# Attention's value product with the values stationary on two halves of the array's columns

## The chip, the cores and the metric

One NeuronCore of a Trainium2 chip runs the kernel. The metric is the device time of one execution in microseconds (us), as a median over several executions. The engines are TensorE (in the rows: PE for matmuls, PEld for weight loads), VectorE (DVE), ScalarE (ACT), GpSimd (POOL) and SyncE (SP, which here issues nearly all DMAs). TensorE's clock has two levels, 1.2 and 2.4 GHz; the rows show the granted share of the full level.

## What is computed

Two layers of a transformer-like block over 256 latent and 256 context tokens, width 1024. Every layer adds the output projection of three groups side by side (a bidirectional gated recurrence, attention, a gated position mixer), then a channel mixer: a dense SwiGLU in the first layer, eight experts, two per token, in the second. The part that is changed is attention with 8 query heads on 2 key-value heads, head size 64, and a sink logit per head:

```python
p = jax.nn.softmax(jnp.concatenate([s_win, s_ctx, s_sink], axis=-1), axis=-1)
p_win = p[..., :n_win].astype(v.dtype)
p_ctx = p[..., n_win:n_win + n_ctx].astype(v.dtype)
o = (jnp.einsum('bnhgqk,bnkhd->bnqhgd', p_win, vw)
     + jnp.einsum('bnhgqc,bchd->bnqhgd', p_ctx, v_ctx))
```

Latent tokens see all context tokens and a window of latent ones; context tokens see context alone, and only the first layer needs their output. All inputs and outputs are f32.

## The kernel before

The kernel is written as Python generators. Each emits instructions for a step and then yields; `run` (line 207) and `weave` (line 223) advance several of them in turn. The emitted order is a priority: a planner of the framework then fixes each engine's queue at compile time, taking by its own estimate what is ready, earlier emitted first. On the chip each queue runs in that order, and semaphores hold what is not yet allowed.

A tile of attention is `attn_tile` (line 1037): 128 query tokens (`tt`) and the four query heads of one key-value head (`g`). Latent tiles have 512 keys in four chunks of 128, context tiles 256 keys in two. Layer 0 has eight tiles: `at0` is group 0 (two context tiles, two latent), `at1` group 1, one after the other, four tiles woven together each. Layer 1 has four, all latent, woven together.

In a tile, each head does this in turn: scores into a PSUM bank (lines 1079 to 1084), the row maximum on VectorE (1085, 1086), Exp with its row sum on ScalarE into the first half of `pt` (1089), the transposes of the head's chunks to another bank (1095), a copy to the second half of `pt` (1097 or 1099), and then one matmul per chunk, with the turned probabilities (128x128) stationary and the values (128x64) moving (1104, by the helper at 1827). The result, tokens by 64 columns a head, collects in `po`. At the end of the tile the four sums are turned to reciprocals (1108 to 1111), `po` is multiplied by them (1114), transposed in two matmuls (1124) and copied into `mix` (1125). f32 matmuls are recorded as two passes each; transposes as one.

Memory of 4 KB per partition is handed out by `Mem` from one first-in-first-out list of 34 slots (`N4`); `room(4, n)` makes a generator yield until n are free. A tile asks for 3 and takes one for `qt`, and for one `pt` per head, which it returns when the head is done. Slots of the recurrence, the output projection and the weight stream come from the same list.

What runs beside the tiles: in layer 0, `hgrn` (the recurrence; its products at line 860 use row halves of the array, its products by decay are lines 849 to 852) and the adaptive-modulation chunks (line 395, four column quarters) run beside `at0`. `filler0` emits the first half of the output projection when recurrence and position mixer are done, and the context half of its second part (`out_proj0`, lines 244 to 246 of `mm3`) when the context tiles are done. In layer 1, `hgrn` runs beside the tiles and `filler1` emits the early output projection (`out_early`) when the recurrence is done and 8 slots are free; `prep_tile` and the expert layer (line 1575) follow. The weights of the experts are prefetched by SP into a ring of slots.

Of the kernel before, what the change touches and what calls it, by code (L numbers as in the profile page):

```python
# [196 lines left out]
class Gen:  # L197
# [839 lines left out]
    def attn_tile(self, l, tt, g):  # L1037
# [32 lines left out]
        pair = (g, tt // 2)  # L1070
        if pair not in st["po"]:
            yield from self.avail("u")
            if pair not in st["po"]:
                st["po"][pair] = [self.psum("u"), 2]
        pb = st["po"][pair]
        po = pb[0][:, 256 * (tt % 2):256 * (tt % 2) + 256]
        for h in range(4):
# [9 lines left out]
            yield from mem.room(4, 1)  # L1087
            pt = mem.get(4, [P, 2, 512], "pp")
            self.act(pt[:, 0, :nk], ps[:, :nk], AF.Exp, bias=nm[:, h:h + 1], accum_out=sm[:, h:h + 1])
            self.done(ps)  # L1090
            yield
            yield from self.avail("t")
            pst = self.psum("t")
            for c in range(nch):
                nc.tensor.transpose(pst[:, c * P:c * P + P], pt[:, 0, c * P:c * P + P], self.ident)
            if h not in PVC[l]:
                self.act(pt[:, 1, :nk], pst[:, :nk], AF.Copy)
            else:
                nc.vector.tensor_copy(pt[:, 1, :nk], pst[:, :nk])
            self.done(pst)  # L1100
            yield
            for c in range(nch):
                vt = st["kv"][:, (k0 // P) + c, 128 + 64 * g:192 + 64 * g]
                self.mm(pb[0], po[:, 64 * h:64 * h + 64], pt[:, 1, c * P:c * P + P], vt, c == 0, c == nch - 1)
            mem.put(pt)
            yield
        mem.put(qt)
        nc.vector.tensor_tensor(es, nm, self.sink[:, l, 4 * g:4 * g + 4], op=ALU.add)
        self.act(es, es, AF.Exp)
        nc.vector.tensor_tensor(es, es, sm, op=ALU.add)  # L1110
        nc.vector.reciprocal(es, es)
        yield from self.mem.room(1, 1)
        o = mem.get(1, [P, 4, 64], "ao")
        nc.vector.tensor_tensor(o, po.rearrange("p (h d) -> p h d", h=4),
                                es[:, :, None].to_broadcast([P, 4, 64]), op=ALU.mult)
        pb[1] -= 1
        if not pb[1]:
            self.done(pb[0])
        yield
        yield from self.avail("t")  # L1120
        pt = self.psum("t")
        of = o.rearrange("p h d -> p (h d)")
# [995 lines left out]
```

## Time and profile before

| | us |
|---|---|
| median of 3 runs | 1839.38 |
| lowest, highest | 1835.87, 1839.55 |
| the profiled execution | 1835.17 |
| its span, first to last instruction | 1833.4 |

The profile is one execution. Its rows give for each group of instructions the busy time and the mean duration of one, for a stretch the busy time of each engine, and in order of time the starts. Durations of matmuls overlap, since the next starts before the last has drained; what a matmul holds TensorE for is read from start to start.

### The profile page before, as it was taken

The page shows a single profiled execution, that of the slowest core. Times are in us where ns is not written, and L with a number is a line of the kernel's source. Part 1 is how long each engine was busy: PE and PEld are TensorE (multiplying, and loading weights), DVE is VectorE, ACT ScalarE, POOL GpSimd, SP SyncE. Part 2 cuts the span into 40 slices and gives each one's busy share as a digit, 9 for nine tenths or more (in the row PEclk, how much of TensorE's full clock was granted, in tenths as well). Part 3 has the DMA queues.
Part 4 walks back from the last instruction along what each step waited for, and adds up shares of the span by engine and source line. Part 5 has one row for each costly group of instructions (what it writes and reads, how often), then busy time and mean ns, then how long its engine had stood idle before and what let it go on. Part 6 is the DMA issues. An engine that isn't in the chain of part 4 may idle for free. (4 is left out here: it accounts for less than half of the span.)

```text
span 1833.4 us, 34728 instructions
## 1 busy us (share of the span) xinstructions
PE 1753.2 (96%) x14056; PEld 1084.3 (59%) x14057; DVE 778.5 (42%) x1924; ACT 537.7 (29%) x1203; POOL 33.3 (2%) x56
## 2 busy tenths in 40 slices
PE   6999999999999999999989998999989999999996
PEld 3999778988788898998843333333333333333332
DVE  4656877899755377868720011110212011120112
ACT  4654655723223256765410010100101011010100
POOL 1000000100000001000000000000000000000000
PEclk9999999999999999999989999999999999999998
DMA  9224342366763245230589999999999999999990
GB/s 347 73 83 147 114 150 80 117 241 226 240 221 134 97 143 182 89 127 13 196 316 379 402 406 407 406 407 400 402 400 406 404 402 402 400 407 404 403 392 31
DMA packets 137006, 485.64 MB, mean 265 GB/s; under 512 B 15888, under 2 KB 17040, under 8 KB 136784
## 3 DMA queue, kind: packets, MB, share of 16 engines
q1 hardware_dynamic: 136080, 480.08, 69.1%
q8 instruction: 168, 2.75, 0.6%
q0 software_dynamic: 704, 2.36, 0.4%
q14 instruction: 54, 0.44, 0.1%
HBM read 481.33 MB, written 1.05 MB: 263 GB/s over the span
## 5 line engine op out<-in xcount | busy, mean ns | idle before, releaser
L1575 PE MATMUL u<-wr,xg 128*32 128x512 f32 (+1 forms) x5376 | 523.9, 545 | 19.7 <-issue 14.6
L1575 PEld LDWEIGHTS u<-wr,xg 128*32 128x32 f32 x5376 | 174.0, 111 | 342.2 <-issue 291.5
L1575 PE MATMUL mm<-wr,mT 128*32 128x512 f32 x2352 | 261.1, 593 | 3.8 <-ACT mh L264 1.5
L125 ACT ACTIVATE hi<-raw 128x512 fp32r<-128x512 f32 (+2 forms) x296 | 160.3, 580 | 247.1 <-PE u L246 84.8
L126 DVE TENSOR_TENSOR lo<-raw,hi 128x512 fp32r<-128x512 f32 (+2 forms) x296 | 178.9, 636 | 98.3 <-ACT hi L125 96.7
L1608 DVE TENSOR_TENSOR mh<-mh,u 128x512 f32<-128x512 f32 (+1 forms) x32 | 19.8, 619 | 410.9 <-PE u L1575 257.0
L1575 PEld LDWEIGHTS mm<-wr,mT 128*32 128x32 f32 x2352 | 77.8, 110 | 175.4 <-issue 149.7
L264 ACT ACTIVATE mh<-u 128x512 f32<-128x512 f32 (+1 forms) x64 | 34.6, 540 | 413.9 <-PE u L1575 413.3
L244 PE MATMUL u<-hx,hi 128*128 128x512 f32 (+1 forms) x384 | 142.9, 372 | 0.0
L245 PE MATMUL u<-hx,lo 128*128 128x512 f32 (+1 forms) x384 | 142.7, 372 | 0.0
L246 PE MATMUL u<-hx,hi 128*128 128x512 f32 (+1 forms) x384 | 142.7, 372 | 0.0
L264 ACT ACTIVATE mT<-t 128x512 f32<-128x512 f32 (+1 forms) x32 | 17.4, 544 | 256.3 <-PE t L1620 255.4
L245 PE MATMUL mm<-fx,lo 128*128 128x256 f32 (+1 forms) x264 | 85.7, 325 | 4.4 <-DVE lo L126 4.2
L244 PE MATMUL mm<-hi,hx 128*128 128x256 f32 x288 | 85.3, 297 | 4.2 <-ACT hx L264 3.9
L244 PE MATMUL mm<-fx,hi 128*128 128x256 f32 (+1 forms) x264 | 85.0, 322 | 0.6 <-ACT hi L125 0.6
L1626 DVE COPY mT<-t 128x256 f32<-128x256 f32 (+1 forms) x32 | 12.5, 392 | 170.6 <-PE t L1625 170.6
L246 PE MATMUL mm<-fx,hi 128*128 128x256 f32 (+1 forms) x264 | 84.6, 321 | 0.0
L245 PE MATMUL mm<-hi,hx 128*128 128x256 f32 x288 | 82.0, 286 | 0.6 <-DVE hx L521 0.3
L246 PE MATMUL mm<-lo,hx 128*128 128x256 f32 x288 | 81.7, 285 | 0.2 <-DVE lo L126 0.2
L246 PEld LDWEIGHTS u<-hx,hi 128*128 128x128 f32 x384 | 72.4, 188 | 12.6
L245 PEld LDWEIGHTS u<-hx,lo 128*128 128x128 f32 x384 | 72.4, 188 | 12.4
L244 PEld LDWEIGHTS u<-hx,hi 128*128 128x128 f32 x384 | 72.4, 188 | 12.4
(342 smaller groups left out, 2624.9 us busy)
## 6 DMA issues: line engine op xcount, KB each, us to landing
wr<-in_moe_g SPq DMA_DIRECT2D x224, 512.0 KB, 10.1
wr<-in_moe_u SPq DMA_DIRECT2D x224, 512.0 KB, 10.1
wr<-in_moe_d SPq DMA_DIRECT2D x224, 512.0 KB, 10.1
adat<-in_w_adaT SPq DMA_DIRECT2D x56, 512.0 KB, 5.0
raw<-in_ffn_gu SPq DMA_DIRECT2D x44, 512.0 KB, 3.5
adaw<-in_w_ada SPq DMA_DIRECT2D x40, 512.0 KB, 6.5
raw<-in_w_in SPq DMA_DIRECT2D x40, 512.0 KB, 3.5
raw<-in_ffn_d SPq DMA_DIRECT2D x24, 384.0 KB, 3.6
```

Of the source, the lines that this page charges most:

```text
L125: nc.scalar.activation(h[:, s], r[:, s], AF.Copy)
L126: nc.vector.tensor_tensor(l[:, s], r[:, s], h[:, s].bitcast(F32), op=ALU.subtract)
L244: i = mm(ps, lh, rh, start=start, stop=False, skip_group_check=True)
L245: mm(ps, ll, rh, start=False, stop=False, skip_group_check=True)
L246: self.final = mm(ps, lh, rl, start=False, stop=stop, skip_group_check=True)
L264: i = self.nc.scalar.activation(out, in_, func, **kw)
L1575: self.nc.tensor.matmul(bank[c:c + 32, :n], lhsT, rhs, start=start, stop=stop, tile_position=(0, c), skip_group_check=True)
L1608: nc.vector.tensor_tensor(h[:, 0, :n], h[:, 0, :n], U[:, :n], op=ALU.mult)
L1626: nc.vector.tensor_copy(hT[:, :m, :, 64:], pt[:, :m * 64].rearrange("p (j a s) -> p j a s", j=m, a=2))
```

## The change

The probabilities are normalised before the product: after every second head the two reciprocals are formed, and GpSimd multiplies the two heads' probabilities by them. The probabilities of all four heads stay (`pp`, two slots). Then, by chunk of keys, the four heads' 128x128 blocks are transposed into one bank and copied to one half of `pT`. After every two chunks two matmuls follow, each with a chunk's values (128x64) stationary and 512 moving columns (four heads by 128 tokens): one on the left half of the array's columns, one on the right, so that even chunks collect in partitions 0 to 63 of `po` and odd ones in 64 to 127. At the end the two halves are added: ScalarE copies each to the other's partitions, VectorE adds, straight into `mix`. The closing multiply and transposes are gone. A tile asks for two slots for `pp` before its first head, returns `qt` after its last and takes one for `pT`, and returns all three at the end. Its steps are 12 turns from the first scores for a latent tile and 9 for a context tile, where both had 14.

```diff
@@ -1067,13 +1067,8 @@
-        pair = (g, tt // 2)
-        if pair not in st["po"]:
-            yield from self.avail("u")
-            if pair not in st["po"]:
-                st["po"][pair] = [self.psum("u"), 2]
-        pb = st["po"][pair]
-        po = pb[0][:, 256 * (tt % 2):256 * (tt % 2) + 256]
+        yield from mem.room(4, 2)
+        pp = [mem.get(4, [P, 2, 512], "pp") for _ in range(2)]
         for h in range(4):
...
-            yield from mem.room(4, 1)
-            pt = mem.get(4, [P, 2, 512], "pp")
-            self.act(pt[:, 0, :nk], ps[:, :nk], AF.Exp, bias=nm[:, h:h + 1], accum_out=sm[:, h:h + 1])
+            p = pp[h // 2][:, h % 2, :nk]
+            self.act(p, ps[:, :nk], AF.Exp, bias=nm[:, h:h + 1], accum_out=sm[:, h:h + 1])
             self.done(ps)
-            yield
+            if h % 2:
+                e = slice(h - 1, h + 1)
+                nc.vector.tensor_tensor(es[:, e], nm[:, e], self.sink[:, l, 4 * g + h - 1:4 * g + h + 1], op=ALU.add)
+                self.act(es[:, e], es[:, e], AF.Exp)
+                nc.vector.tensor_tensor(es[:, e], es[:, e], sm[:, e], op=ALU.add)
+                nc.vector.reciprocal(es[:, e], es[:, e])
+                for i in range(2):
+                    x = pp[h // 2][:, i, :nk]
+                    nc.gpsimd.tensor_scalar(x, x, es[:, h - 1 + i:h + i], None, op0=ALU.mult)
+            yield
+        mem.put(qt)
+        pT = mem.get(4, [P, 2, 512], "pT")
+        yield
+        po = None
+        for c in range(nch):
             yield from self.avail("t")
-            pst = self.psum("t")
-            for c in range(nch):
-                nc.tensor.transpose(pst[:, c * P:c * P + P], pt[:, 0, c * P:c * P + P], self.ident)
-            if h not in PVC[l]:
-                self.act(pt[:, 1, :nk], pst[:, :nk], AF.Copy)
+            ps = self.psum("t")
+            for h in range(4):
+                nc.tensor.transpose(ps[:, h * P:h * P + P], pp[h // 2][:, h % 2, c * P:c * P + P], self.ident)
+            if c not in PVC[l]:
+                self.act(pT[:, c % 2], ps, AF.Copy)
             else:
-                nc.vector.tensor_copy(pt[:, 1, :nk], pst[:, :nk])
-            self.done(pst)
-            yield
-            for c in range(nch):
-                vt = st["kv"][:, (k0 // P) + c, 128 + 64 * g:192 + 64 * g]
-                self.mm(pb[0], po[:, 64 * h:64 * h + 64], pt[:, 1, c * P:c * P + P], vt, c == 0, c == nch - 1)
-            mem.put(pt)
-            yield
-        mem.put(qt)
...
-        nc.vector.tensor_tensor(o, po.rearrange("p (h d) -> p h d", h=4),
-                                es[:, :, None].to_broadcast([P, 4, 64]), op=ALU.mult)
...
-        for j in range(2):
-            nc.tensor.transpose(pt[:, j * P:j * P + P], of[:, j * P:j * P + P], self.ident)
-        self.to_mix(2 * g, tt, pt)
+                nc.vector.tensor_copy(pT[:, c % 2], ps)
+            self.done(ps)
+            yield
+            if c % 2 == 0:
+                continue
+            if po is None:
+                po = yield from self.either("mm", "u")
+            for i in range(2):
+                v = st["kv"][:, (k0 // P) + c - 1 + i, 128 + 64 * g:192 + 64 * g]
+                nc.tensor.matmul(po[64 * i:64 * i + 64], v, pT[:, i], start=c == 1, stop=c == nch - 1,
+                                 tile_position=(0, 64 * i), skip_group_check=True)
+            yield
+        mem.put(pT, *pp)
...
+        for i in range(2):
+            self.act(o[64 * i:64 * i + 64], pv[64 - 64 * i:128 - 64 * i, :, i], AF.Copy)
+        for i in range(2):
+            r = slice(64 * i, 64 * i + 64)
+            nc.vector.tensor_tensor(self.mix[g][r, :, ts], pv[r, :, i], o[r], op=ALU.add)
+        self.done(po)
```

## Rows read from the trace of the kernel before

**Rows 1.** The page, busy time: engine, us, share of the span, instructions.

```profile
PE 1753.2 (96%) x14056; PEld 1084.3 (59%) x14057; DVE 778.5 (42%) x1924; ACT 537.7 (29%) x1203; POOL 33.3 (2%) x56
```

**Rows 2.** Windows with changed tiles: stretch, length, busy by engine; PEclk, DMA share, GB/s.

```profile
213.00:263.00 50.00, 49.37 (x376) 42.20 (x377) 39.80 (x154) 26.22 (x70) 0.56 (x2) 1.00 0.34 115
296.50:322.50 26.00, 25.31 (x204) 23.44 (x203) 19.50 (x64) 21.64 (x65) 0.00 (x0) 1.00 0.18 61
835.60:880.00 44.40, 44.40 (x357) 38.61 (x356) 36.72 (x119) 18.82 (x46) 0.56 (x2) 1.00 0.04 13
880.00:902.50 22.50, 21.80 (x137) 18.66 (x135) 18.29 (x50) 13.69 (x36) 0.00 (x0) 1.00 0.62 219
```

**Rows 3.** Windows: the end of the prefetch, and a stretch of the expert layer.

```profile
930.00:940.00 10.00, 9.23 (x67) 6.27 (x69) 1.11 (x4) 3.49 (x9) 0.00 (x0) 0.95 0.57 227
...
1000.00:1100.00 100.00, 95.61 (x946) 36.52 (x942) 12.07 (x19) 11.30 (x24) 0.00 (x0) 1.00 1.02 402
```

**Rows 4.** Timeline of PE, layer 1: start, us, instructions. Projection, then attention.

```profile
883.80 0.48 PE L244 MATMUL u<-hi,mx 128*128 128x512 f32 x1
...
897.32 1.00 PE L1827 MATMUL u<-akv,pp 128*128 128x64 f32 x8
```

**Rows 5.** The tile `pp`: the value products, ns min/median/max, first and last start.

```profile
L1827 PE MATMUL u<-akv,pp x320: 217/275/323, 220.3 to 901.3; 128*128 128x64 f32 x160
```

**Rows 6.** Timeline of PE: sixteen passes of value products and what follows.

```profile
258.83 2.00 PE L1827 MATMUL u<-akv,pp 128*128 128x64 f32 x16
260.67 0.66 PE L1827 MATMUL u<-S,QC 128*128 128x128 f32 x4
```

**Rows 7.** Timeline of PE: transposes, and products on row halves (L860), apart and together.

```profile
255.34 0.71 PE L860 MATMUL u<-Bl,Al 64*128 64x128 f32 x4
255.98 0.66 PE L1095 MATMUL t<-ident,pp 128*128 128x128 f32 x4
256.56 0.71 PE L860 MATMUL u<-Bl,Al 64*128 64x128 f32 x4
...
859.62 0.72 PE L860 MATMUL u<-Bl,Al 64*128 64x128 f32 x8
860.27 0.50 PE L1079 MATMUL mm<-KT,qt 128*128 128x512 f32 x1
```

**Rows 8.** Timeline of PE in three narrow windows: modulation on four column quarters.

```profile
262.55 0.64 PE L395 MATMUL u<-adaw,sil 128*32 128x512 f32 x4
...
263.00 1.46 PE L395 MATMUL u<-adaw,sil 128*32 128x512 f32 x8
...
263.43 1.03 PE L395 MATMUL u<-adaw,sil 128*32 128x512 f32 x4
```

**Rows 9.** The tile `ao`: the closing multiply, ns min/median/max.

```profile
L1114 DVE TENSOR_TENSOR ao<-u,aes x12: 414/424/426, 259.9 to 901.7; 128x256 f32<-128x256 f32 x12
```

**Rows 10.** Groups by line on POOL: shape, count, busy us, mean ns, idle before.

```profile
L517 POOL TENSOR_TENSOR nt<-X,ny 128x512 f32<-128x512 f32 x4 | 5.0, 1263 | 8.6 <-ACT adas L264 8.6
...
L337 POOL CAST Mf<-cld 128x1024 fp32r<-128x1024 f32 x1 | 1.0, 1042 | 0.9 <-DMA cld<-in_Mf 0.9
```

**Rows 11.** Groups by line on DVE, 835 to 880 us: attention's, and a product by decay.

```profile
L1085 DVE TENSOR_REDUCE anm<-mm 128x1 f32<-128x512 f32 x13 | 8.8, 686 | 0.8 <-PE mm L1083 0.7
L1099 DVE COPY pp<-t 128x512 f32<-128x512 f32 x7 | 4.8, 687 | 1.1 <-PE t L1095 1.0
...
L851 DVE TENSOR_TENSOR Bl<-E,Tq 128x128 f32<-128x128 f32 x11 | 3.2, 289 | 0.0
```

**Rows 12.** Timelines of DVE and POOL, 337.5 to 343.2 us: additions beside POOL.

```profile
338.63 0.96 DVE L477 TENSOR_TENSOR nsq<-nsq 128x256 f32<-128x256 f32 x1
...
342.65 0.41 DVE L477 TENSOR_TENSOR nsq<-nsq 128x256 f32<-128x256 f32 x1
...
338.20 3.58 POOL L517 TENSOR_TENSOR nt<-X,ny 128x256 f32<-128x256 f32 x4 [9.93 <-DVE ny L497]
```

More of the change, by code (lines that the diff above doesn't have):

```diff
@@ new lines, in attn_tile @@
+            yield
[4 more added lines that the diff above has]
+        for c in range(nch):
+            yield from self.avail("t")
+            ps = self.psum("t")
[3 more added lines that the diff above has]
+                self.act(pT[:, c % 2], ps, AF.Copy)
+            else:
+                nc.vector.tensor_copy(pT[:, c % 2], ps)
@@ L1090, in attn_tile @@
             self.done(ps)
             yield
-            yield from self.avail("t")
-            pst = self.psum("t")
-            for c in range(nch):
-                nc.tensor.transpose(pst[:, c * P:c * P + P], pt[:, 0, c * P:c * P + P], self.ident)
-            if h not in PVC[l]:
-                self.act(pt[:, 1, :nk], pst[:, :nk], AF.Copy)
-            else:
-                nc.vector.tensor_copy(pt[:, 1, :nk], pst[:, :nk])
-            self.done(pst)
-            yield
-            for c in range(nch):
-                vt = st["kv"][:, (k0 // P) + c, 128 + 64 * g:192 + 64 * g]
-                self.mm(pb[0], po[:, 64 * h:64 * h + 64], pt[:, 1, c * P:c * P + P], vt, c == 0, c == nch - 1)
@@ L1105, in attn_tile @@
-            mem.put(pt)
-            yield
-        mem.put(qt)
[L1108 to L1113, printed above, removed]
-        nc.vector.tensor_tensor(o, po.rearrange("p (h d) -> p h d", h=4),
-                                es[:, :, None].to_broadcast([P, 4, 64]), op=ALU.mult)
@@ L1116, in attn_tile @@
-        pb[1] -= 1
-        if not pb[1]:
-            self.done(pb[0])
-        yield
-        yield from self.avail("t")
-        pt = self.psum("t")
-        of = o.rearrange("p h d -> p (h d)")
-        for j in range(2):
-            nc.tensor.transpose(pt[:, j * P:j * P + P], of[:, j * P:j * P + P], self.ident)
-        self.to_mix(2 * g, tt, pt)
+            if c % 2 == 0:
[6 more added lines that the diff above has]
+                                 tile_position=(0, 64 * i), skip_group_check=True)
@@ new lines, in attn_tile @@
+            yield
+        mem.put(pT, *pp)
+        yield from mem.room(1, 1)
+        o = mem.get(1, [P, 2, P], "ao")
+        pv = po.rearrange("p (k h t) -> p k h t", k=2, h=2)
+        ts = slice(tt * P, tt * P + P)
+        for i in range(2):
[3 more added lines that the diff above has]
+            nc.vector.tensor_tensor(self.mix[g][r, :, ts], pv[r, :, i], o[r], op=ALU.add)
```

## The prediction

> **What bounds the kernel now.** I began with the busy times: TensorE is busy 96% of the span [rows 1]. Then I cut the run into stages. Those with the changed tiles, 213 to 263, 296.5 to 322.5 and 835.6 to 902.5, have TensorE busy for all but 2.0 of 142.9 us, at the full granted clock, while VectorE and ScalarE are below 85% [rows 2]. So TensorE time taken out there is worth its full length, as long as other ready work closes up behind it. From 936 us on the expert layer runs at over 400 GB/s with the DMA engines full [rows 3]; it has none of the changed code and only moves as a block. Its prefetch is no obstacle to an earlier start: in 930 to 940 the DMA share falls to 0.57, because the slots are full and wait for the first matmuls [rows 3]. An earlier start frees them earlier.
>
> The changed code is twelve tiles (eight of four key chunks, four of two). They run in three stages: group 0 of layer 0 among the recurrence (213 to 263), group 1 of layer 0 nearly alone (296.5 to 322.5), and layer 1's four (835.6 to 902.5), first among its recurrence and then beside the early output projection, whose matmuls run from 883.80 to 897.32 with little between [rows 2, 4].
>
> **TensorE, part by part.** Removed: 160 products of 64 columns, recorded as 320 passes [rows 5]. Sixteen passes start at 258.83 and the next work at 260.67, so a pass costs 0.115 us [rows 6]: 36.8 us. Also gone are 24 transposes of `ao`, two a tile; four such transposes hold TensorE from 255.98 to 256.56 [rows 7], 0.145 us each, 3.5 us: together 40.3 us.
>
> Added: 40 products with 512 moving columns, in 20 pairs on the two column halves. The nearest rows are the adaptive-modulation products on four column quarters, also 512 f32 columns: four records start together at 262.55, the next at 263.00, then at 263.43 [rows 8]. So one round of different products lasts 0.43 us whatever their number, and a product takes two rounds: 0.86 us for a pair side by side, 1.72 us if the halves took turns.
>
> Entering and leaving a divided array costs something too. The recurrence's products on two row halves take 0.65 us from the first start to the next work when both halves stand together (859.62 to 860.27) and 0.64 us when the planner queued one half alone (255.34 to 255.98) [rows 7]. Four passes of 128 columns, each a quarter of the 0.43 us of [rows 8], would be 0.43, so the visit adds 0.2, and a half queued alone saves nothing. The Trainium skill (TensorEngine Tiling (Array Packing), Key Properties) says that a change of tiling mode drains TensorE; by that rule the price of the visit belongs to each pair, and the trace agrees with 0.2 us.
>
> A pair is therefore 1.06 us, twenty are 21.2 us, and the net is 40.3 - 21.2 = 19.1 us less on TensorE: 5.8 in each stage of layer 0 (48 products and 8 transposes, 12.2, against 6 pairs, 6.4) and 7.4 in layer 1 (64 and 8, 15.9, against 8 pairs, 8.5). If halves took turns the net would be 17.2 us smaller, 1.9. The 160 transposes of probabilities stay, regrouped by chunk.
>
> **The other engines.** Per tile ScalarE gets a second small Exp and two shifted copies of 64x256 for one 128x256 copy; VectorE gets six small steps for three and two 64x256 additions for one 128x256 multiply. The multiply that goes takes 0.42 us [rows 9]; with two additions as long in its place, and the small steps, I take 0.9 us more a tile on VectorE and 0.6 on ScalarE (bounds 0.4 and 1.5). In the mixed stages other work hides it; in the 26 us stage, where ScalarE is busy 21.6 us and VectorE 19.5 [rows 2], four tiles add 2 to 4 us, still under the old length.
>
> GpSimd gets 48 multiplications by a column. None is in the trace. Above lies the two-input multiply of 512 columns at 1.26 us, below half of a 1024-column cast, 0.52 us [rows 10]. It reads one tile like the cast, so I take 0.65 for 512 columns and 0.4 for 256: about 27 us in all on an engine that is otherwise idle. Its queue also holds four state clears of the recurrence and the small loads; a multiplication queued behind a clear that waits for its slot would hold up the tile. No DMA is issued by the changed steps themselves.
>
> **Where TensorE will find nothing to do.** The new order has a longer chain: nothing of a tile can be transposed until all four heads are normalised, and `pT` has room for two chunks, so the third chunk's copy waits for the first pair's product. A tile's tail becomes: reciprocal, two GpSimd products (1.3 us), transposes, copy, pair, copy, pair, copies, additions, some 7 us against about 3.5 (estimates from the durations above). What hides it differs by stage.
>
> Layer 0, group 0: the free 4 KB slots, counted through the code's takes and returns, are exactly 8 when the tiles begin, so all four get their two. They need 12 or 9 turns each where they needed 14, end about 14 turns before the recurrence instead of with it, and leave the recurrence's last turns with less beside them. Of the 5.8 us saved here I take 2 back (0 to 5).
>
> Layer 0, group 1: it starts those turns earlier, so that about 7 of its 16 heads are queued beside the dense output projection's first part, and its own tail has the context half of the second part beside it. Again I take 2 of 5.8 back (0 to 6).
>
> Layer 1: here the slots bite. Three are free when the tiles reach the softmax. Until now each tile took one and gave it back per head, so three of four went on together. Now one tile takes two, the three others wait for two, and the first gives back only at its end. The others begin when the recurrence returns its slots near its end; and the early output projection, which asks for eight free slots, is queued only after two of the late tiles are done instead of amid them. The 44.4 us of the recurrence stage [rows 2] lose most of their filling. They can't shrink as much as that work, for the recurrence is a chain through VectorE: of its 36.7 busy us [rows 2], attention's reductions and copies are 8.8 + 4.8 [rows 11], so 23 us stay, and 10 or so of attention's will be fitted in. I expect this stage to end near 39 us after its start, with 8 to 10 us of TensorE idle, and the stored-up work (three tiles' transposes and pairs, 13, and the projection, some 11) to run dense after it. Of 7.4 us saved in layer 1, I take 9 back: 1.6 us lost. If the planner can draw the late tiles' scores forward, the idle time falls to 3; if not, it is 16.
>
> Pairs drawn apart: the first product of a pair is ready when its chunk is copied, some 0.4 us before the second, and the planner orders each engine by readiness. A pair wholly apart costs 1.06 us more [rows 7]. I put it at 2 us in all (0 to 10).
>
> **The sum.** -19.1 + 2 + 2 + 9 + 2 = -4.1 us. The profiled execution took 1835.2 us (span 1833.4), so 1831.1 by the sum. The median of the three runs, 1839.4, is 4.2 us above that execution; on its level the forecast is 1835.3 us, a gain of 0.2%, at the edge of what can be told. 0.2% (3.7 us) is about what a measurement of this kernel can tell from no change.
>
> **Rivals.** First, *all of it arrives*: the planner draws scores forward and TensorE stays filled in layer 1 as now. For it: no wait of note on TensorE in the mixers now. Against it: the slot count. Idle and pairs apart 3 instead of 15: 19.1 - 3 = 16.1 us less, 1823.
>
> Second, *layer 1 starves and GpSimd holds up VectorE* (the slower side). Place: the recurrence of layer 1. While GpSimd's multiply of two tiles ran, from 338.20 to 341.78, VectorE's addition of two tiles took 0.96 us; just after, the same line took 0.41 [rows 12]. The recurrence's products by decay, 0.29 us each [rows 11], all read two tiles. Price: 16 multiplications of 0.65 us in layer 1, about half meeting such an instruction, 5 us on the chain, and TensorE idle 16 instead of 9: -4.1 + 7 + 5 = +7.9, 1847. It decides against the change once idle time and hold-up together pass 19.1 us. The Trainium skill (SBUF — State Buffer, Who interferes with whom) has the rule: VectorE with two SBUF inputs and GpSimd reading SBUF exclude each other for a whole instruction. By that rule all 48 could cost up to 27 us of VectorE; the rows here agree that the blocked instruction waits, with 0.55 us.
>
> Third, *the halves take turns*: the change doesn't do what it says. The rounds of [rows 8] speak against it, though for quarters. 17.2 us more than forecast, less some 3 us of idle time that it would fill: +10, about 1849.
>
> **How the numbers follow.** Forecast (1829 to 1842): 0.47. All arrives (1818 to 1829): 0.20. Starved and held up (1842 to 1853): 0.26. Turns: 0.07. Faster by over 0.2% is under 1835.7: 0.20 and about half of the forecast, together 0.42. Slower is over 1843.1: the last two but for the second's mildest part, 0.31. The rest, 0.27, is within. The range leaves out the ends of the first and of the last two: 1822 to 1851.
>
> **What would show it.** Two records of 512 columns starting within 0.05 us, and pairs of 0.86 us, show the halves working together; 1.7 us show turns. TensorE busy in the recurrence stage of layer 1 well below 44 of 44 shows the starving; its length shows whether the recurrence is a chain or was held by TensorE. VectorE's products by decay far above 0.29 us while GpSimd multiplies show the hold-up. The last attention step of layer 0 relative to the output projection shows the earlier start. The prediction is wrong in its mechanism if the stage of layer 1 stays filled, or if the expert layer doesn't move with the start of its first matmul.

## The result: slower, and the profile after

The changed kernel takes 1860.95 us (median of five runs, 1856.01 to 1861.53) where the kernel before takes 1838.19 in the same comparison: a ratio of 1.0114, 95% interval 1.0098 to 1.0131, about 21 us slower by the ratio and 22.8 between the two medians. The forecast was 1835.3 and the range ended at 1851. The profiled execution took 1856.30 us (span 1854.2; before 1833.4).

The page's busy times of the changed kernel, against [rows 1]:

```profile
span 1854.2 us, 34353 instructions
...
PE 1758.4 (95%) x13792; PEld 1057.0 (57%) x13793; DVE 787.3 (42%) x1972; ACT 543.1 (29%) x1219; POOL 98.9 (5%) x104
```

GpSimd (POOL) has 98.9 us where it had 33.3. The same four stretches as [rows 2] in the changed kernel (windows; busy time of each engine, granted TensorE clock, DMA share, GB/s):

```profile
213.00:263.00 50.00, 46.55 (x305) 33.06 (x304) 43.99 (x174) 29.10 (x78) 20.66 (x18) 0.97 0.34 117
296.50:322.50 26.00, 18.16 (x73) 10.02 (x72) 16.20 (x60) 13.91 (x43) 20.07 (x16) 0.80 0.12 42
835.60:880.00 44.40, 42.92 (x332) 34.46 (x331) 40.95 (x162) 24.80 (x61) 6.87 (x6) 1.00 0.04 13
880.00:902.50 22.50, 15.44 (x49) 8.71 (x49) 11.45 (x41) 8.99 (x29) 19.10 (x12) 0.62 0.20 70
```

TensorE, which had 2.0 us of idle time in all of them, now lacks 7.84 us in the second and 7.06 in the fourth, and there its granted clock is 0.80 and 0.62 on average, that is, at half speed (1.2 GHz) for part of the time. In both GpSimd is the engine that is busy.

The whole of the two stages, from layer 0's first score to its first down-projection matmul and from layer 1's first score to the first expert matmul. First the kernel before:

```profile
211.40:468.00 256.60, 254.09 (x1576) 218.43 (x1575) 220.05 (x548) 122.61 (x289) 8.91 (x12) 1.00 0.46 157
835.70:936.30 100.60, 94.34 (x632) 81.31 (x632) 74.65 (x238) 42.42 (x110) 0.56 (x2) 0.95 0.46 168
```

then the changed one:

```profile
211.70:477.30 265.60, 252.77 (x1417) 200.38 (x1415) 227.60 (x580) 125.69 (x296) 49.07 (x44) 0.97 0.44 152
845.40:961.50 116.10, 101.12 (x530) 71.45 (x529) 77.66 (x254) 44.93 (x120) 25.97 (x18) 0.87 0.38 145
```

These four rows are the account on which the rest stands. The length of a stage is TensorE's *idle* time (length less busy) and its busy time; the busy time times the granted clock is the *work* at full clock, and what is left was *lost to half clock*. Summed over windows of 5 us, which follow the clock more closely than one mean, both stages together have:

| | work | idle | half clock | first expert matmul |
|---|---|---|---|---|
| before | 344.8 | 8.8 | 3.6 | 936.3 |
| changed | 337.6 | 27.8 | 16.2 | 961.5 |
| difference | -7.2 | +19.0 | +12.6 | +25.2 |

So TensorE does have less to do, though by 7 us and not by 19, and the gain and more is waited away. (The 0.8 us between the sum and 25.2 lie before and between the stages.) Layer 0 loses 9.0 of it, layer 1 15.5.

The expert layer passes the delay on. Weight loads of 512 KB issued up to 1000 us, before (DMA issues, 700 to 1000 us):

```profile
wr<-in_moe_g SPq DMA_DIRECT2D x28, 512.0 KB, 7.5
wr<-in_moe_u SPq DMA_DIRECT2D x28, 512.0 KB, 6.2
...
wr<-in_moe_d SPq DMA_DIRECT2D x18, 512.0 KB, 7.5
```

and in the changed kernel:

```profile
wr<-in_moe_g SPq DMA_DIRECT2D x24, 512.0 KB, 7.7
wr<-in_moe_u SPq DMA_DIRECT2D x22, 512.0 KB, 6.3
...
wr<-in_moe_d SPq DMA_DIRECT2D x8, 512.0 KB, 7.2
```

54 instead of 74; at the 402 GB/s of [rows 3] a load lasts 1.30 us, so 20 are 26 us. The last expert matmul starts 22.0 us later (1836.6 against 1814.6).

GpSimd's part, by shape (line, engine, operation, tiles, shapes, count, busy us, mean ns):

```profile
L1093 POOL TENSOR_SCALAR pp<-pp,aes 128x512 f32<-128x512 f32 x32 | 51.0, 1607 | 73.2 <-DVE Al L849 57.5 <-DVE aes L1090 12.9 <-ACT E L264 1.9
L1093 POOL TENSOR_SCALAR pp<-pp,aes 128x256 f32<-128x256 f32 x16 | 14.6, 928 | 59.5 <-DVE anm L1081 37.2 <-DVE aes L1090 18.8 <-PE mm L1078 1.8
```

A multiplication of 512 columns takes 1.61 us and one of 256 0.93: 65.6 us. Who waited for that line (us, times), and TensorE's longest wait between 180 and 970 us (us in total, times, longest):

```profile
who waited for it (us, times):
  PEld t L1103: 24.8, 24
  PE t L1103: 16.3, 20
...
PE t L1103 <- POOL pp L1093: 16.3, 20, 5.3
```

The waiting line is the transposes of the normalised probabilities. Before, no wait in these stages was longer than 2.1 us.

### The profile page after: what moved, and what is told of

Read it like the earlier page. It is cut to its first block, busy times and chain, and to the rows that moved or that the text cites. A ratio compares the mean times of both kernels' runs of the same rounds, so it can differ in the third digit from the quotient of the medians.

```text
span 1854.2 us, 34353 instructions
## 1 busy us (share of the span) xinstructions
PE 1758.4 (95%) x13792; PEld 1057.0 (57%) x13793; DVE 787.3 (42%) x1972; ACT 543.1 (29%) x1219; POOL 98.9 (5%) x104
## 5 line engine op out<-in xcount | busy, mean ns | idle before, releaser
L264 ACT ACTIVATE mT<-t 128x512 f32<-128x512 f32 (+1 forms) x32 | 17.4, 544 | 254.2 <-PE t L1624 253.2
L1630 DVE COPY mT<-t 128x256 f32<-128x256 f32 (+1 forms) x32 | 12.5, 391 | 168.5 <-PE t L1629 168.5
L246 PEld LDWEIGHTS u<-hx,hi 128*128 128x128 f32 x384 | 72.2, 188 | 12.6
L245 PEld LDWEIGHTS u<-hx,lo 128*128 128x128 f32 x384 | 72.3, 188 | 12.4
```

Of the source, the lines that this page charges most:

```text
L245: mm(ps, ll, rh, start=False, stop=False, skip_group_check=True)
L246: self.final = mm(ps, lh, rl, start=False, stop=stop, skip_group_check=True)
L264: i = self.nc.scalar.activation(out, in_, func, **kw)
L1630: nc.vector.tensor_copy(hT[:, :m, :, 64:], pt[:, :m * 64].rearrange("p (j a s) -> p j a s", j=m, a=2))
```

## Experiments

All kernels are compared with the kernel before on the same chip. Since the expert layer after the change differs between kernels for reasons of its own (below), the first expert matmul of the profiled execution is the better measure of the attention stages. It comes from one execution of each kernel, and so do work, idle time and half clock. Most of these executions lie within 3 us of the median beside them, but before's is 3 to 4 us below, the changed kernel's 4.7 below, e17's 6.5 below and e18's 7.0 above, so differences of a few us between such columns say little. Kernels with another number of slots have another order from the start, so their stages aren't cut as above. In the diffs `...` stands for lines left out.

| kernel | us | ratio (95%) | work | idle + half clock | first expert matmul |
|---|---|---|---|---|---|
| before | 1838 to 1839 | | 344.8 | 12.4 | 936.3 |
| changed | 1861.0 | 1.0114 (1.0098-1.0131) | 337.6 | 44.0 | 961.5 |
| e1 no multiply | 1829.7 | 0.9947 (0.9930-0.9963) | 333.2 | 25.3 | 941.1 |
| e2 multiply on VectorE | 1854.5 | 1.0083 (1.0066-1.0100) | 334.9 | 38.8 | 958.7 |
| e4 pairs together | 1854.9 | 1.0089 (1.0072-1.0106) | 327.4 | 51.2 | 959.3 |
| e5 VectorE, pairs | 1844.9 | 1.0024 (1.0012-1.0036) | 328.8 | 37.5 | 946.8 |
| e10 split, pairs | 1842.2 | 1.0022 (1.0007-1.0038) | 329.5 | 36.3 | 945.4 |
| e11 ScalarE, pairs | 1845.9 | 1.0044 (1.0029-1.0058) | 332.1 | 34.9 | 949.7 |
| e13 no multiply, pairs | 1821.3 | 0.9909 (0.9875-0.9943) | 327.8 | 25.3 | 935.5 |
| e17 three engines, pairs | 1841.4 | 1.0014 (1.0002-1.0027) | 327.7 | 32.7 | 939.6 |
| e14 the same, 36 slots | 1833.6 | 0.9974 (0.9965-0.9984) | | | 936.8 |

Theories: A, GpSimd's multiply is slow and every tile waits for it; B, layer 1 starves for 4 KB slots; C, pairs drawn apart and half clock.

**e1: no multiply.**

```diff
-                for i in range(2):
-                    x = pp[h // 2][:, i, :nk]
-                    nc.gpsimd.tensor_scalar(x, x, es[:, h - 1 + i:h + i], None, op0=ALU.mult)
```

> The 48 multiplications on GpSimd are left out (the probabilities stay unnormalised), all else stays; the span of the changed kernel is 1854.2 us, of the one before 1833.4. Theory A, the multiply itself: each of 512 columns holds GpSimd 1.56 us instead of the 0.65 of the prediction, and tiles wait in its queue; without it the three attention stages close up and the time falls by 18 to 28 us, to 1833 to 1843, with value products of group 1 ending before 322 and the first expert matmul before 943. Theory B, the room in layer 1: the slots stay as they are, so of the 15.7 us lost in layer 1 at least 10 stay; only the 9.5 us of layer 0 go, to about 1850. Theory C, pairs apart and half clock: 9 of 20 pairs stay apart and the time falls by under 8 us, to 1853 or more.

The first expert matmul comes at 941.1, 20.4 us earlier. The expert line's source view (count, ns min/median/max, first and last start) says why the time of 1829.7 must not be read as it stands; first e1, then the changed kernel:

```profile
L1576 PE MATMUL u<-wr,xg x5120: 376/592/1062, 941.1 to 1790.0; 128*32 128x512 f32 x149, 128*32 128x256 f32 x48
L1576 PE MATMUL mm<-wr,mT x2240: 589/592/618, 984.6 to 1807.6; 128*32 128x512 f32 x187
```

```profile
L1579 PE MATMUL u<-wr,xg x5376: 376/592/1061, 961.5 to 1820.3; 128*32 128x512 f32 x150, 128*32 128x256 f32 x50
L1579 PE MATMUL mm<-wr,mT x2352: 589/592/617, 1005.0 to 1836.6; 128*32 128x512 f32 x196
```

Unnormalised probabilities change the routing, and the expert layer has 368 fewer of these matmuls. Theory A holds for 20.4 of the 25.2 us, with one reservation: with the multiplication the wait of the transposes for the reciprocals is gone too. Even so the kernel without the multiply is 4.8 us behind before at that point.

**e2: the multiply on VectorE.**

```diff
-                    nc.gpsimd.tensor_scalar(x, x, es[:, h - 1 + i:h + i], None, op0=ALU.mult)
+                    nc.vector.tensor_scalar(x, x, es[:, h - 1 + i:h + i], None, op0=ALU.mult)
```

> The same 48 multiplications, by VectorE instead of GpSimd. Theory A: VectorE's operations of 512 columns take 0.69 us in the trace of the changed kernel, so a multiplication is 0.69 us at most against 1.56; most of the loss goes, 1836 to 1846, unless VectorE becomes the bound of the 26 us stage (it was busy 19.5 there and gets up to 8 more). Theory B: about 1852, since the slots don't change. Theory C: within 5 us of the changed kernel, 1856 to 1861.

A miss for theory A: 1854.5, though a multiplication takes 0.48 us there (0.35 for 256 columns). The first expert matmul comes 2.8 us earlier than with GpSimd and 17.6 later than without the multiplication, so GpSimd's slowness alone isn't the cause. The number is near theory B's, but e5 and the stretches under it point to another cause.

**e3 and e8: the changed tile in one layer alone.** e8 has `l == 1` in the same line.

```diff
-        unit = lambda tt, g: self.attn_tile(l, tt, g)
+        unit = lambda tt, g: (self.attn_tile if l == 0 else self.attn_tile_old)(l, tt, g)
```

> The changed tile in layer 0 alone, with GpSimd's multiply; layer 1 has the tile of before. The expert layer's first matmul was 9.5 us late from layer 0 and 15.7 more from layer 1. Theory A: 32 of the 48 multiplications stay (37 of 65 us of GpSimd), layer 0 keeps its loss of about 9 and the time is 1845 to 1850. Theory B, layer 1 by its slots being the main loss: the same here, so this run says how much each layer costs; if layer 1 alone were at fault through a later start it would give under 1842.

> The changed tile in layer 1 alone, layer 0 as before. In the changed kernel layer 1 took 116.1 us from its first score to the first expert matmul where it took 100.6 before (90.0 work, 15.0 idle, 11.1 half clock against 90.7, 6.3, 3.6). If the two layers' losses are independent: first score at the old 835.7 within 2, first expert matmul near 952, time 1846 to 1853. If much of the loss of layer 1 came from layer 0 (slots handed over late), the first expert matmul is before 945.

Each layer loses by itself. In e3 layer 0 is 9.5 us late at the down projection (477.5 against 468.0), as in the changed kernel, and the first expert matmul 14.0. In e8 layer 1 takes 114.0 us from its first score to the first expert matmul, 13.4 more than before, and its first score is 4.1 us late, outside the 2 allowed; 953.8 in all against the 952 expected. Its time of 1857.0 misses the 1846 to 1853: its expert layer, from first to last matmul, takes 884.2 us where before took 878.3. The two losses, 14.0 and 17.5 us, don't add up to the 25.2 of both layers together. e3's time of 1877.3 was expected by neither theory: its expert layer, with the same matmuls, runs 905.1 us from its first to its last where before had 878.3. More on that below.

**e4: pairs together.**

```diff
-            for i in range(2):
+            ms = {}
+            for i in (1, 0):
...
+            self.after(ms[0], ms[1])
```

> The two products of a pair are ordered so that the first to be queued is the one whose chunk is copied last; the other has to follow it. GpSimd's multiply stays. Theory C: all or nearly all of 20 pairs stand side by side (9 stood apart), L1116 busy falls from 32.3 us to about 21, and the time falls by 9 x 1.06 = 9.5 us, to about 1851. Theory A: TensorE waits for GpSimd in these stages anyway, so the time falls by under 4 us, to 1857 or more. A pair may also come later as a whole, which gives some of it back in either theory.

The products' busy time by tile (groups by line, 200 to 950 us), changed and then e4:

```profile
L1116 PE MATMUL mm<-pT,akv 128*64 128x512 f32 x40 | 20.4, 656 | 0.1
L1116 PE MATMUL u<-pT,akv 128*64 128x512 f32 x40 | 15.4, 633 | 0.0
```

```profile
L1117 PE MATMUL mm<-pT,akv 128*64 128x512 f32 x40 | 13.5, 702 | 0.2 <-ACT pT L264 0.2
L1117 PE MATMUL u<-pT,akv 128*64 128x512 f32 x40 | 11.1, 655 | 0.0
```

35.8 us become 24.6; in the timeline 19 of the 20 pairs now stand together, where 11 did. TensorE's work falls by 10.2 us to 327.4, 17.4 under before. But the idle and half-clock time rises by 7.2, and the first expert matmul gains 2.2: while GpSimd holds the tiles up, time saved on TensorE is spent waiting. That is theory A's reading; the time of 1854.9 lies between what the two theories had (1851, and 1857 or more).

**e5: both.**

> The multiply on VectorE and the pairs ordered to stand together, both at once. From the first score of layer 0 to the first down-projection matmul and from the first score of layer 1 to the first expert matmul, TensorE's time is the sum of work (busy time at full clock), idle time and time lost to half clock: before 344.8 + 8.8 + 3.6, changed 337.6 + 27.8 + 16.2, multiply on VectorE alone 334.9 + 25.2 + 13.6, pairs alone 327.4 + 29.6 + 21.6. If the two causes are separate, work falls to 325 to 328 and idle and clock stay near 25 + 14, 366 in all, 9 us over before: 1842 to 1849. If ordering the pairs only turns work into waiting, as it mostly did alone, the time stays at 1852 to 1856.

1844.9, as expected: work 328.8, idle and half clock 37.5. The pairs that gave 2.2 us beside GpSimd give 11.9 with the multiply on VectorE (958.7 to 946.8). What is left is seen in three stretches and the one behind the second (windows of e5):

```profile
231.00:241.00 10.00, 6.38 (x37) 4.83 (x37) 9.95 (x42) 2.50 (x12) 0.00 (x0) 0.75 0.01 2
...
301.00:311.00 10.00, 5.06 (x23) 3.20 (x22) 9.74 (x46) 7.37 (x27) 0.00 (x0) 0.83 0.00 1
...
321.00:331.00 10.00, 10.00 (x80) 9.05 (x79) 6.59 (x16) 5.90 (x14) 0.00 (x0) 1.00 0.31 107
...
875.00:885.00 10.00, 6.41 (x25) 3.79 (x24) 9.91 (x42) 6.87 (x23) 0.00 (x0) 0.80 0.21 76
```

First VectorE is full and TensorE half empty, then TensorE is full and VectorE at two thirds: the tiles' score steps come in a block, and their transposes and products in a block behind it.

**e10, e11 and e15: less on VectorE.** All three have the pairs together. e10 multiplies each second head on ScalarE (`self.act(x, x, AF.Copy, scale=...)`) and the others on VectorE, e11 all of them on ScalarE; e15 is e10 with 36 slots and all copies of turned probabilities on ScalarE:

```diff
-PVC = ((0,), (0, 2))
+PVC = ((), ())
```

> Pairs ordered to stand together, and of the 48 multiplications 24 on VectorE and 24 on ScalarE, none on GpSimd. With all on VectorE (1844.9 us) three stretches of 10 us had VectorE busy 9.95, 9.74 and 9.91 and TensorE only 6.38, 5.06 and 6.41 (231 to 241, 301 to 311, 875 to 885), while ScalarE had 2.5, 7.4 and 6.9. Theory, VectorE is the bound of these stretches: half of its 20.7 us of multiplications gone gives TensorE 6 to 10 us of idle and half-clock time back, 1835 to 1840. Rival, the chain behind the fourth head sets them whatever engine multiplies: within 3 us of 1844.9.

> The same with all 48 multiplications on ScalarE. ScalarE's operation of 512 columns takes 0.6 us here (0.4 for 256), so 26 us more on it. If VectorE was the bound: as good as the split in the stages with the recurrence, and in group 1 of layer 0, alone for 26 us with ScalarE at 21.6 of it already before the change, a few us worse; 1836 to 1844. If the chain sets them: 1843 to 1850.

> The split with 36 slots, and all copies of turned probabilities on ScalarE; 16 of 40 were on VectorE, 0.69 us each, 11 us in all. If VectorE's load is what remains: 1832 to 1838, and stretches with VectorE over 9.5 of 10 us become fewer. If it is the chain of steps: within 2 us of 1839.9; if ScalarE is now the late one, 1842 to 1848.

1842.2, 1845.9 and 1843.9: the rivals' numbers (for e15 those of a late ScalarE). That VectorE alone is the bound falls: with half of the multiplications moved the first expert matmul gains 1.4 us, and in e15 it stands at 943.9 where its fellow e12 (below) has 943.1. What the multiply doesn't ask of one engine it seems to ask of the next; that is a reading of these times and not shown.

**e6 and e7: two heads at a time,** e6 with VectorE, e7 with GpSimd.

```diff
+        for hp in range(2):
+            yield from mem.room(4, 2)
+            pp = mem.get(4, [P, 2, 512], "pp")
+            for h in (2 * hp, 2 * hp + 1):
...
+            for b in range(nch // 2):
...
+                for i in range(2):
+                    nc.tensor.matmul(po[64 * i:64 * i + 64, :256], v, pT[:, b, 256 * i:256 * i + 256], ...)
...
+            mem.put(pT, pp)
```

> Two heads at a time: one probability slot a tile instead of two, 40 pairs of 256 columns instead of 20 of 512, both products of a pair behind one copy, multiply on VectorE, the slots given back after each two heads. Theory, the chain behind the fourth head and the room in layer 1 leave TensorE idle and so at half clock: work 345 - 40.3 + 40 x (0.43 + 0.2) = 330, idle and clock near 12 + 5 instead of 25 + 14, first expert matmul 5 to 12 us before the old 936, time 1824 to 1834, better than both kernels. Rival, the multiplication itself is what costs wherever it stands (VectorE gets 21 us more, and more small steps): idle and clock stay at 35 to 40 and the time is 1848 to 1858.

> The same with the multiply on GpSimd: 48 multiplications of 1.56 and 0.92 us, 65 us, remain, but two heads' multiplications (3.1 us) stand between a tile's scores and its transposes instead of up to sixteen in a row. If the order of the tile is the cause: within 8 us of its fellow with VectorE. If GpSimd's rate is: 15 us or more above it, since four tiles need 25 us of GpSimd in a stage of 26.

Both far off: 1903.2 and 1945.1. The finer grain didn't fill TensorE (e6: work 336.2, idle and half clock 48.3, first expert matmul 964.3), and GpSimd makes 43 us of difference (1007.6), with TensorE waiting 22.0 us in 33 waits for its multiply. So it isn't enough to divide the tile. e6 loses another 41 us in the expert layer (919.2 us long). TensorE's waits there (1000 to 1800 us; us in total, times, longest), before and then e6:

```profile
PE u L1575 <- issue: 14.2, 11, 3.4
```

```profile
PE u L1580 <- issue: 23.8, 13, 3.7
PE mm L1580 <- issue: 15.9, 8, 3.0
PE mm L1580 <- DMA wr<-in_moe_d: 9.6, 4, 2.5
```

The same matmuls, with the same number of slots, have 25 us more of waits for which the trace has no releaser. In e6 they recur at the same steps of each pair of experts (2.7, 3.4 and 3.7 us at 1080.0, 1309.2 and 1538.6). Why stays open.

**e9, e12 and e16: two more slots.**

```diff
-N4, N2, N1 = 34, 12, 24
-N4B = 16
+N4, N2, N1 = 36, 10, 20
+N4B = 14
```

> The changed kernel as it is, with GpSimd's multiply, but 36 slots of 4 KB instead of 34 (ten 2 KB and twenty 1 KB slots instead of twelve and twenty-four; the expert layer has the same number of slots as before). In layer 1 five slots are free when the first tile reaches its softmax, so two of the four tiles go on at once where it was one. Theory B, the room in layer 1 is what starves it: the stage from layer 1's first score to the first expert matmul falls from 116.1 us to 104 to 109, GpSimd's run of twelve multiplications begins earlier, and the time falls by 6 to 12 us, to 1849 to 1855. Theory A, GpSimd's 1.56 us a multiplication: 16 of them are 25 us wherever they stand, and the stage stays within 4 us of 116; 1857 or more.

> The split with 36 slots of 4 KB instead of 34, as above. With the multiply cheap the room in layer 1 should now show more than beside GpSimd: theory B, the stage of layer 1 (106.3 us with all on VectorE) falls to 95 to 99 and the kernel is 5 to 9 us under the split with 34; it then beats the kernel before. If room isn't what starves it, within 3 us of the split.

> The kernel before with 36 slots of 4 KB (ten of 2 KB, twenty of 1 KB), the control for the kernels with 36. TensorE was 96% busy and waited for no slot of note: within 3 us of 1838.5. If it is faster by more, the gain of e12 over e10 says nothing on the changed tile.

e9, the changed kernel with 36 slots, is no faster against before (1858.7, 1.0116), and its first expert matmul is later (965.3; the stage of layer 1 takes 122.2 us, more than either theory had). e12 is 2.3 us under e10 at that point, within the 3 us that stood against theory B, and 1839.9 in time, level with before (1.0012, 0.9999 to 1.0026). But the control spoils the test: the kernel before, with nothing changed but the slots, takes 1860.9, and its first expert matmul moves from 936.3 to 962.1. The number of slots reorders all of the mixers, and that costs as much as the whole change under study. Theory B has nothing for it in e9, and can't be ruled out by it either.

**e13: no multiply, pairs together.**

> No multiply at all (probabilities stay unnormalised) and pairs ordered to stand together, 34 slots. Without the normalisation the routing differs and the expert layer has fewer matmuls (7392 instead of 7752 in the kernel that left out the multiply alone), so it is read at the first expert matmul: 936.3 before, 941.1 without the multiply alone. If the multiply and the pairs apart are the whole loss, TensorE's work to there is about 325 against 344.8, idle and half clock 20 to 25 against 12.4, and the first expert matmul stands at 927 to 933. If the tile's new order costs time by itself (all four heads, then transposes, then copies and pairs), work saved turns into waiting: 936 to 942.

935.5, between the two cases and half a us short of the second. The multiply (with its wait for the reciprocals) and the pairs explain all of the loss: 25.2 us turn to -0.8. But of the 17.0 us of work that TensorE is spared no more than that arrives: idle and half clock are 25.3 against 12.4, and the stretch between the layers is 3.3 us longer. Windows of e13:

```profile
296.00:311.00 15.00, 12.70 (x63) 7.99 (x62) 13.44 (x55) 13.67 (x44) 0.00 (x0) 0.89 0.18 55
311.00:326.00 15.00, 15.00 (x113) 12.68 (x113) 10.79 (x25) 9.28 (x22) 0.00 (x0) 1.00 0.17 60
```

The block of scores (VectorE 13.4 and ScalarE 13.7 of 15) and the block of products behind it are there without any multiply. I put that down to the order, four heads first and then transposes by chunk; no run changes the order alone, and the room is as tight as in the changed kernel, so it is not shown.

**e14, e17 and e18: three engines.** e14 (36 slots) and e17 (34) give GpSimd the first head of each tile, VectorE the third, ScalarE the other two; e18 gives GpSimd the first two (36 slots).

```diff
+                    if i:
+                        self.act(x, x, AF.Copy, scale=es[:, h - 1 + i:h + i])
+                    else:
+                        (nc.gpsimd if h == 1 else nc.vector).tensor_scalar(...)
```

> Pairs together, 36 slots, and the multiplications of a tile's four heads on GpSimd, ScalarE, VectorE and ScalarE: GpSimd only gets the first head's, which is wanted last of all, 12 in all. Against the split with 36 slots (1839.9) VectorE loses 12 of 24 multiplications, 5.6 us. If VectorE's load is what remains: 1833 to 1838. If GpSimd's 1.56 us still delays the tile's transposes: 1841 to 1848.

> The three-engine kernel with the 34 slots of before. If 36 slots helped the changed tile: 1836 to 1842 (the split went from 1842.2 to 1839.9 with 36). If they cost it what they cost the old kernel, or part of it: under 1832. First expert matmul before 936.8 in the second case.

> As the three-engine kernel with 36 slots (1833.6), but GpSimd multiplies the first two heads of each tile, 24 in all, ScalarE and VectorE 12 each. If GpSimd's cost is its place in the chain, the last heads' multiplications before the transposes: within 3 us of 1833.6, or better, since ScalarE is relieved of 6 us. If its rate sets the pace (eight multiplications of 1.4 us a stage of four tiles): 1839 to 1848.

e14 beats both kernels: 1833.6, 0.9974 (0.9965 to 0.9984), though not in the stages under study, since its expert layer starts at 936.8 where before had 936.3; what it gains lies behind that point. e17 is 1841.4, no better than the split on two engines (e10), though its profiled execution, the fastest of twelve, has the first expert matmul 5.8 us earlier than e10's. e18 is 1848.0, 14.4 us behind e14. Who waited for GpSimd's multiplications, in e14 (us, times):

```profile
  PEld t L1106: 1.7, 1
  PE t L1106: 1.5, 1
```

and in e18, with their duration by shape:

```profile
L1094 POOL TENSOR_SCALAR pp<-pp,aes 128x512 f32<-128x512 f32 x16 | 26.7, 1681 | 58.7 <-DVE aes L1090 24.0 <-DVE anm L1081 23.8 <-ACT hosq L264 10.9
...
  PEld t L1108: 8.2, 7
  PE t L1108: 6.7, 7
```

With one head a tile TensorE hardly waits for GpSimd, with two it does, though these are the first two heads'. So it isn't only the place behind the last head that costs: four tiles ask for eight multiplications, of 1.68 us each where they have 512 columns, in one stage. The direct waits are smaller than the 14 us; how much of the rest is the other order isn't settled, nor why 36 slots help the three-engine kernel by 8 us and cost the kernel before 23.

## Why the prediction was wrong, step by step

Forecast and measurement can be laid side by side term by term. The sum had -4.1 us, the first expert matmul is 25.2 late: 29.3 us apart. Work accounts for 9.9 of it (-19.1 + 2 forecast, -7.2 measured), idle time for 6.0 (13 and 19.0), half clock for 12.6 (nothing and 12.6), the stretches outside the two stages for 0.8.

**TensorE's work: right, once the pairs stand together.** 40.3 - 21.2 = 19.1 us less was forecast; e4 measures 17.4 with 19 of 20 pairs together, e13 17.0. The halves do work side by side (timeline of the changed kernel; start, us, count):

```profile
249.76 1.08 PE L1116 MATMUL mm<-pT,akv 128*64 128x512 f32 x4
250.67 0.60 PE L1116 MATMUL u<-pT,akv 128*64 128x512 f32 x2
```

The four records are one pair (two products of two passes each), and the next pair starts 0.91 us after the first: two rounds, not four. *The halves take turns* falls.

**Pairs drawn apart: mis-sized.** 2 us were taken, with 10 as the bound. 9 of 20 pairs were apart, as here with a block of the recurrence between the products:

```profile
862.94 1.07 PE L1116 MATMUL mm<-pT,akv 128*64 128x512 f32 x2
863.94 0.72 PE L860 MATMUL u<-Bl,Al 64*128 64x128 f32 x8
864.59 1.07 PE L1116 MATMUL mm<-pT,akv 128*64 128x512 f32 x2
```

and e4 puts their work at 10.2 us (e4 brings 8 of the 9 together, 8 times the 1.06 of the working is 8.5). The reason had been given (the planner orders by readiness, and the copies are 0.4 us apart); I should have counted pairs as apart unless something holds them together.

**GpSimd's multiply: the step that failed.** It was priced at 0.65 and 0.4 us because it reads one tile like the cast of [rows 10]; it takes 1.61 and 0.93, 65.6 us in all instead of 27. At 512 columns that is above the two-input multiply that was the upper bound (1.26 in [rows 10], 1.27 in the trace after), at 256 level with it (0.94). The number of tiles read isn't what sets GpSimd's time here. The Trainium skill (GPSIMD Engine Reference, Elementwise — side-by-side cycle accounting) has some 1.8 cycles an element as GpSimd's best case, 0.77 us for 512 columns, and 2.6 measured for two inputs. The rows differ and decide: a column costs (1.607 - 0.928) / 256 = 2.7 ns here, and 512 cost twice the page's best case.

The price is only part of the error. VectorE does the same multiplication in 0.48 us, less than the 0.65 of the sum, and the first expert matmul is still 17.6 us behind the kernel without it (e2 against e1), or 11.3 with the pairs together (e5 against e13). From GpSimd to VectorE it gains 2.8 us, or 12.5 with the pairs together. So a cheaper multiplication on a busier engine still costs about half as much or more; one of 0.65 us on GpSimd was not tried. The sum had no term at all for a step that is put between a tile's scores and its transposes. How its cost divides into the multiplying engine's load, the wait for the reciprocals and the order is open.

**"An engine that is otherwise idle": the second half of that step.** The 27 us were laid beside other work. But the four tiles' multiplications come together, 16 in group 1 (GpSimd 20.07 of 26 us), 12 in layer 1 (19.10 of 22.5). The prediction had no transpose of a tile start before its last multiplication. The trace shows the transposes of a tile's first chunk released head by head, with TensorE waiting 0.7 to 1.2 us for each (timeline of the changed kernel):

```profile
881.86 0.33 PE L1103 MATMUL t<-ident,pp 128*128 128x128 f32 x1 [0.74 <-POOL pp L1093]
...
883.40 0.33 PE L1103 MATMUL t<-ident,pp 128*128 128x128 f32 x1 [0.99 <-POOL pp L1093]
...
886.48 0.48 PE L1103 MATMUL t<-ident,pp 128*128 128x128 f32 x1 [1.21 <-POOL pp L1093]
```

The chunk's copy, which needs a block of each head, comes after the last. An engine that is idle on average is no cover if all its work comes at once. Leaving the multiplication out (e1) gives back 20.4 us of the 25.2.

**Idle time: 13 us forecast, 19.0 measured.** 4 against 10.3 in layer 0, 9 against 8.7 in layer 1. The second is the right size by luck, for the mechanism was wrong. The prediction had TensorE idle 8 to 10 us within layer 1's recurrence, which was to shrink from 44 to about 39 us and no further since it was a chain through VectorE, and dense work behind it. From layer 1's first score to the recurrence's last matmul, before and then changed (windows):

```profile
835.70:879.70 44.00, 44.00 (x353) 38.21 (x353) 36.51 (x119) 18.72 (x44) 0.56 (x2) 1.00 0.04 13
```

```profile
845.40:875.90 30.50, 29.48 (x234) 22.70 (x234) 27.76 (x100) 11.84 (x28) 6.87 (x6) 1.00 0.05 19
```

The stretch shrinks to 30.5 us with TensorE filled (1.0 us idle), so the chain through VectorE is not what had held it at 44, and the other 14.0 us of idle time come behind it. By the prediction's own sign, a recurrence stage that stays filled, its mechanism was wrong. The first tile does go alone, as the slot count said, and the three others' scores come in a block behind, from 866.8 to 887.7, and their twelve multiplications run from 880.2 to 899.9 with one gap of 0.5 us. But without the multiply the excess idle time of layer 1 is 3.0 us (9.3 against 6.3), with the slots as few as ever. Whether the room has a part in what remains is open, since 36 slots reorder everything.

**Half clock: not in the sum at all.** 12.6 us, more than any idle term of the sum. The stretches in which TensorE lacks work have the low clock too: 0.80 from 296.5 to 322.5, 0.62 from 880 to 902.5, where both had been 1.00 [rows 2]. A forecast of idle time on TensorE needs this second term. The rows of before gave one hint of it: 0.95 from 930 to 940, where TensorE had 9.23 of 10 us [rows 3]; in all, the kernel before lost 3.6 us so.

**The slower rival named the right stages and the wrong price.** *Layer 1 starves and GpSimd holds up VectorE* was worth 1847. The hold-up is seen, but far too small to matter (VectorE, groups by line, 853 to 862 us, where GpSimd multiplies the first tile of layer 1):

```profile
L850 DVE TENSOR_TENSOR Al<-E,Tkb 128x128 f32<-128x128 f32 x4 | 1.3, 336 | 0.0
...
L849 DVE TENSOR_TENSOR Al<-E,Tkf 128x128 f32<-128x128 f32 x4 | 1.3, 319 | 0.0
L852 DVE TENSOR_TENSOR Bl<-E,Tq 128x128 f32<-128x128 f32 x3 | 0.8, 283 | 0.0
L851 DVE TENSOR_TENSOR Bl<-E,Tq 128x128 f32<-128x128 f32 x3 | 0.8, 276 | 0.0
```

Against the 0.289 us of [rows 11] these fourteen lose some 0.25 us together where 5 were forecast; the longest took 0.49. GpSimd was busy for 6 of those 9 us. The twelve other multiplications of layer 1 came after the recurrence's last product by decay (869.5 us) and met none. In the whole trace 28 such products overlap a multiplication; 23 took 0.29 us or less, the longest 0.81, and all together lose 1.4 us. The Trainium skill (SBUF — State Buffer, Who interferes with whom) calls the port pair that VectorE shares with GpSimd an exclusive lock, and has a VectorE instruction with two SBUF inputs contend with a GpSimd instruction that reads SBUF. The trace agrees that some instructions are held, but none for anything like the 1.6 us of a multiplication.

**The expert layer moves with its first matmul: right here, not in general.** 25.2 us late at the start, 22.0 at the last matmul. In e3 and e6 the layer itself grew by 27 and 41 us.

*All of it arrives* fell with the idle time.

## What to carry to other kernels

Price an operation on GpSimd from the same operation, or not at all: reading less than its neighbour in the trace doesn't make it cheaper. A step that is put between two others needs a term of its own in the sum even where its engine is idle, and what comes in one burst ahead of a stage's critical step needs cover in that burst, not on average. When TensorE is relieved by an order with fewer and larger steps, ask what it does while the other engines prepare them; here even a free multiply left the gain of 17 us waited away, part of it as half clock. And where a planner orders the queues, an edit that adds or frees room can move as much time as the change that one studies (23 us in e16): such a control belongs into the plan from the start.

## What the runs showed of the hardware that was not expected

- GpSimd's multiplication by a column, in place, f32: 1.61 us for 512 columns and 0.93 for 256; VectorE's 0.48 and 0.35.
- Products on two column halves overlap when they are queued next to each other (0.91 us for a pair, 1.00 for one product alone), and a pair with other work between its products costs more: TensorE's work fell by 10.2 us when 8 more pairs stood together.
- The same expert layer, matmul for matmul, lasts between 873 and 920 us in different kernels (e3's four times lie between 1875.5 and 1882.4, so it is the kernel's), with waits of 1 to 4 us on TensorE that the trace puts down to nothing.
